# Second FFN: seven products for eight in the down projection, and low parts of weights made by transfers

## The chip, the cores and the metric

The kernel runs on one core of a Trainium2 chip. The metric is the device time of one execution in microseconds (us), the median of three runs. TensorE (PE) multiplies, VectorE (DVE) and ScalarE (ACT) work on tiles in SBUF and PSUM, GpSimd (POOL) works on SBUF tiles and issues transfers, and SyncE (SP) issues transfers.

## The reference, cut to what matters

One decoder layer on 544 tokens (a prompt of 512 and 8 x 4 sample tokens), all in float32, width 1024, hidden width 2816:

```python
def swiglu(x, w_gate, w_up, w_down):
    return (jax.nn.silu(x @ w_gate) * (x @ w_up)) @ w_down

x = x + 0.5 * swiglu(rms_norm(x, ffn1_norm), ffn1_gate, ffn1_up, ffn1_down)
z = rms_norm(x, mix_norm) @ w_in          # split among the heads of two mixers
x = x + concat(attention(z), gated_recurrence(z)) @ w_out
x = x + 0.5 * swiglu(rms_norm(x, ffn2_norm), ffn2_gate, ffn2_up, ffn2_down)
```

The attention is block-sparse, over a paged cache for the sample tokens (its pages are gathered by indirect transfers); the recurrence is computed in chunks.

## The kernel before, in words

Activations lie transposed: 8 tiles of 128 features x 544 tokens (`x` in the first FFN, `y` in the second), in two halves of 272 columns. A float32 product is made of three matmuls on rounded parts: every operand is split in a high part `hi` (a cast on ACT) and a low part `lo = src - hi` (a subtraction on DVE), and hi x hi, hi x lo and lo x hi are summed in PSUM (`products`). A matmul always has 128 rows, 128 columns of weights and 272 columns of tokens.

Weights come as jobs, in the order in which the products need them (`weight_jobs`). `w_load` loads raw pieces of 4 x 128 x 128 (256 KB; 192 KB where a group has 6 tiles) on SP's queue into slots `raw`, and `w_split` makes units (a pair `whi`, `wlo`) of them, at most `AHEAD` = 4 ahead of the products. There are 4 raw slots and 4 slots for pairs, and more from the time when the activations' own parts `xh`, `xl` are free (`more_slots`).

An FFN has 22 tiles of hidden features f, in groups of 8, 8 and 6 (`FGROUPS`). For f under 5 (`NREG`) gate and up are plain products: 8 k-tiles x 3 matmuls x 2 halves each, 48 matmuls. From f = 5 on, gate and up of one f are the two columns of a 2 x 2 block product, and seven products replace eight (`paired_gemm`; weights' sums `S`, two of them on DVE and two on POOL; token sums `xwh`, `xwl` made once by `right_factors`). Each of the seven takes 4 k-tiles x 3 matmuls, 84 matmuls for an f. After every group the down projection runs plainly over the group's hidden tiles (`hidden`, `split_hidden`: parts `hh`, `hl` or `xh`, `xl`), for 8 output tiles m in two halves, and adds half of the result to x. The last group's additions are followed by the output's transposes and stores (`store`).

Between the FFNs stand the 28 input projections (`project`), the mixers, and 8 output projections, whose weights come by the same jobs.

The order of instructions on each engine is written out before the kernel runs: `Order` holds a price for every instruction and transfer, gives each a planned start, and sorts every engine's queue by these starts (`give_out`). Each engine then works its queue strictly in that order and waits where an operand is late. All instructions are recorded by one helper, so the profile's line is always L284, and tiles' names tell them apart. In the second FFN the hidden parts and the extra weight slots share the names `xh` and `xl`.

At the start of the second FFN the residual `y` is read back from DRAM (`xs`) by eight transfers that POOL issues.

Of the kernel before, what the change touches and what calls it, by code (L numbers as in the profile page):

```python
# [30 lines left out]
FGROUPS = ((0, 8), (8, 8), (16, 6))  # L31
# [22 lines left out]
PACE = 0.8  # L54
# [124 lines left out]
class Engine:  # L179
# [22 lines left out]
    def __getattr__(self, op):  # L202
        real = getattr(self.real, op)

        def call(*args, **kw):
            names = list(self.tensors(args, kw))
            if op == "dma_start":
                s = self.order.dma(self.part, 4 * args[1].shape[0] * self.free(args[1]), names)
# [45 lines left out]
class Order:  # L254
# [103 lines left out]
    def dma(self, part, size, names, cost=0.06):  # L358
        s = self.fit(part, self.start(part, names), cost)
        e = self.fit("dma", s + cost + 1.5, size / 330e3) + size / 330e3  # L360
# [51 lines left out]

class Build:
# [34 lines left out]

    def weight_jobs(self):
# [7 lines left out]
        def plain(m, nk, r0, c0):  # L457
            out.append({"paired": False, "src": quarters(m, nk, r0, c0), "nk": nk // 2, "raw": [], "done": 0})

        def ffn(p):  # L460
            gate, up, down = (a[p + n][0] for n in ("_gate", "_up", "_down"))
            for g0, ng in FGROUPS:
                for f in range(g0, g0 + ng):
                    if f < NREG:
                        plain(gate, KD, 0, 128 * f)
                        plain(up, KD, 0, 128 * f)
                    else:
                        out.append({"paired": True, "nk": KD // 2, "raw": [], "done": 0,
                                    "src": quarters(gate, KD, 0, 128 * f) + quarters(up, KD, 0, 128 * f)})
                for m in range(KD):  # L470
                    plain(down, ng, g0, 128 * m)

        ffn("ffn1")
        for n, j in IN_ORDER:
            plain(a["w_in"][0], KD, 0, COLS[n] + 128 * j)
        for m in range(KD):
            plain(a["w_out"][0], KD, 0, 128 * m)
        ffn("ffn2")
        return out

    def room(self, kind, job):

        free = [x for x in self.slots[kind] if x["used"] < x["bufs"] and (x["extra"] is None or job["paired"])]
# [13 lines left out]
    def more_slots(self, pool):  # L497

        for i in range(KD):
            if i < 2:  # L500
                for t in ("xh", "xl"):
                    self.slots["raw"].append({"pool": pool, "tags": (f"{t}{i}",), "bufs": 1, "used": 0, "freed": [],
                                              "extra": pool})
            else:
                self.slots["w"].append({"pool": pool, "tags": (f"xh{i}", f"xl{i}"), "bufs": 1, "used": 0,
                                        "freed": [], "extra": pool})
# [9 lines left out]
    def w_load(self):  # L516
# [7 lines left out]
        self.nc.sync.dma_start(raw[:, :job["nk"]], job["src"][len(job["raw"])])  # L524
# [5 lines left out]
    def split_unit(self, src, nk, x):  # L530
        nc = self.nc
        hi, lo = self.take_slot(x, (F32R, F32R))
        nc.scalar.copy(hi[:, :nk], src[:, :nk])
        nc.vector.tensor_tensor(lo[:, :nk], src[:, :nk], hi[:, :nk].bitcast(F32), op=ALU.subtract)
        return hi, lo, x

    def w_split(self):
# [4 lines left out]
        if len(job["raw"]) <= (3 if job["paired"] else n):  # L542
            return False
        x = self.room("w", job)
        if x is None:
            return False
        nk = job["nk"]
        if job["paired"]:
            (a11, a12, a21, a22) = (r for r, _ in job["raw"])
            if n == 0:  # L550
                S = [self.tl(self.sums, [128, 4, 128], f"S{i}") for i in range(4)]
                for i, (e, p, q, op) in enumerate(((self.nc.vector, a21, a22, ALU.add),
                                                   (self.nc.vector, S[0], a11, ALU.subtract),
                                                   (self.nc.gpsimd, a11, a21, ALU.subtract),
                                                   (self.nc.gpsimd, a12, S[1], ALU.subtract))):
                    e.tensor_tensor(S[i][:, :nk], p[:, :nk], q[:, :nk], op=op)
                job["units"] = (a11, S[1], S[0], a12, S[2], S[3], a22)
            src = job["units"][n]
            self.units.append(self.split_unit(src, nk, x))
            drop = {0: (0, 2), 3: (1,), 6: (3,)}.get(n, ())  # L560
        else:
            self.units.append(self.split_unit(job["raw"][n][0], nk, x))
# [9 lines left out]
    def w_pump(self):  # L572
        while (len(self.units) < AHEAD and self.w_split()) or self.w_load():
# [69 lines left out]
    PAIRED = ((0, 0, True), (1, 4, True), (2, 3, True), (0, 1, False), (1, 5, False), (2, 2, False), (1, 6, False))  # L643

    def paired_gemm(self, xw, nk, evacs):
# [6 lines left out]
        for (b, r, first), evac in zip(self.PAIRED, evacs):  # L652
            w, = self.next_w(1)
            for k in range(nk):
                xh, xl = xw[k]
                self.products(ps[b], w, k, xh[:, r], xl[:, r], first and k == 0, k == nk - 1, not first)
# [4 lines left out]
    def right_factors(self, pool, x, gain):  # L661


# [4 lines left out]

        def lows(hi, lo, r, src):
            nc.scalar.copy(hi[:, r], src)  # L670
            nc.vector.tensor_tensor(lo[:, r], src, hi[:, r].bitcast(F32), op=ALU.subtract)

        def diff(out, p, q):
            nc.vector.tensor_tensor(out, p, q, op=ALU.subtract)

        for k in range(n):

            home, th, tl = self.hidden_home
            B1, B2, S1, S2 = [self.tl(home, [128, 2, HT], f"{t}{i}") for i in (6, 7) for t in (th, tl)]
            hi = self.tl(pool, [128, 7, HT], f"xwh{k}", F32R)  # L680
            lo = self.tl(pool, [128, 7, HT], f"xwl{k}", F32R)
            steps = [lambda B=B, m=m: nc.vector.scalar_tensor_tensor(
                B.rearrange("p a b -> p (a b)"), x[m], self.gains[:, gain, m:m + 1], self.R, op0=ALU.mult, op1=ALU.mult)
                for B, m in ((B1, k), (B2, k + n))]
            steps += [lambda a=a: diff(*a) for a in ((S1[:, 0], B1[:, 1], B1[:, 0]), (S1[:, 1], B2[:, 1], S1[:, 0]),
                                                     (S2[:, 0], B2[:, 1], B1[:, 1]), (S2[:, 1], B2[:, 0], S1[:, 1]))]
            steps += [lambda a=a: lows(hi, lo, *a) for a in ((slice(0, 1), B1[:, 0:1]), (slice(1, 3), B2),
                                                             (slice(3, 5), S1), (slice(5, 7), S2))]
            for step in steps:
                step()  # L690
                self.order.t = self.order.free["pe"] + PACE
                yield
            self.xw.append((hi, lo))
# [76 lines left out]

    def hidden(self, pool, i, hs):
# [4 lines left out]
        u = self.tl(pool, [128, T], "t_h", bufs=2)  # L776
# [8 lines left out]
        def up(p, h):  # L785
            c = self.cols(h)
            nc.vector.tensor_tensor(u[:, c], p, s[:, c], op=ALU.mult)
            if h:
                hs[i] = self.split_hidden(u, i)

        return gate, up

    def split_hidden(self, u, i):
        nc = self.nc
        pool, th, tl = self.hidden_home
# [1049 lines left out]
```

## Time and profile before

| what | value |
|---|---|
| median of 3 runs | 1205.38 us (1205.19 to 1206.52) |
| the profiled execution | 1210.65 us, span 1208.9 us |
| granted TensorE clock | 0.990 |
| PE busy | 1178.1 us, 97% of the span |
| DVE busy | 858.5 us, 71% |
| ACT busy | 551.9 us, 46% |
| POOL busy | 228.3 us, 19% |
| moved by DMA | 144.74 MB, mean 120 GB/s |

The span runs from the first to the last instruction of the program; the profiled execution's time has 1.75 us around it. Stages by the trace: first FFN to about 400 us, projections and mixers to about 785 us, output projection to about 826 us, second FFN from there to the end. The busy time of PE is that of pipelined matmuls; what a matmul costs is the distance from one to the next.

### The profile page before, as it was taken

The numbers are of one execution on the slowest core, as the hardware profiler recorded it, in microseconds if no ns is written. First come the engines' busy times: TensorE is split into PE (matmuls) and PEld (weight loads), VectorE is DVE, ScalarE is ACT, GpSimd is POOL, SyncE is SP. The second block draws the span as 40 slices with busy tenths as digits, with TensorE's granted clock in tenths as the row PEclk, the third lists the DMA queues.
The fourth block names the chain that finished last, engine by engine and source line by source line (L and its number), as shares of the span: only waits on it lengthen the run. The fifth ranks groups of instructions, "written<-read, shape, count | busy, mean of one in ns | idle before, by whom it ended". The sixth has DMA issues, their size and how long they took to land.

```text
span 1208.9 us, 26320 instructions
## 1 busy us (share of the span) xinstructions
PE 1178.1 (97%) x10571; PEld 1113.7 (92%) x10571; DVE 858.5 (71%) x1729; ACT 551.9 (46%) x1125; POOL 228.3 (19%) x211
## 2 busy tenths in 40 slices
PE   8999999999999999989999999899999999999998
PEld 8989999999999988878878867799999999999998
DVE  6988559954875698877776557667977488736843
ACT  6455246532654345554556433344554266524632
POOL 3012012200202401000332344220020023102200
PEclk9999999999999999989999999899999999999999
DMA  5244453333314642322565776352344323323222
GB/s 161 79 123 114 133 148 97 97 106 87 87 54 135 193 129 69 97 72 74 181 195 160 235 262 222 111 158 79 93 118 131 97 81 104 106 87 88 63 79 82
DMA packets 216238, 144.74 MB, mean 120 GB/s; under 512 B 12035, under 2 KB 204067, under 8 KB 216116
## 3 DMA queue, kind: packets, MB, share of 16 engines
q1 hardware_dynamic: 205588, 106.60, 30.6%
q0 software_dynamic: 10432, 36.32, 9.1%
q8 instruction: 83, 1.36, 0.5%
q14 instruction: 39, 0.32, 0.1%
q10 hardware_dynamic: 96, 0.14, 0.0%
HBM read 133.94 MB, written 11.83 MB: 121 GB/s over the span
## 4 chain that ended last, share of the span: by engine, by line
PE 77%; DVE 13%; ACT 3%; DMA 3%; issue 2%; SPq 1%; POOL 0%; DVEq 0%; ACTq 0%; POOLq 0%
PE mm L284 51%; PE sm L284 26%; DVE wlo L284 3%; DVE xl L284 2%; DVE xwl L284 1%; DMA raw<-ffn_down 1%; ACT xh L284 1%; DVE t_h L284 1%; SPq L284 1%; ACT whi L284 1%; DVE hl L284 1%; ACT sq L284 1%; DMA raw<-ffn_up 1%; DVE S L284 1%; DMA KV<-cache_v,idx 1%
## 5 line engine op out<-in xcount | busy, mean ns | idle before, releaser
L284 PE MATMUL mm<-xh,whi 128*128 128x272 f32 x1216 | 365.0, 300 | 1.0 <-DVE t_g L284 0.5
L284 PE MATMUL mm<-xl,whi 128*128 128x272 f32 x1216 | 352.4, 290 | 5.4 <-DVE xl L284 5.2
L284 PE MATMUL mm<-xh,wlo 128*128 128x272 f32 x1216 | 353.2, 290 | 1.1 <-DVE wlo L284 1.1
L284 ACT CAST whi<-raw 128x512 fp32r<-128x512 f32 (+1 forms) x230 | 138.7, 604 | 261.4 <-PE mm L284 192.3
L284 PEld LDWEIGHTS mm<-xh,whi 128*128 128x128 f32 x1216 | 231.5, 190 | 18.2 <-issue 15.7
L284 PEld LDWEIGHTS mm<-xl,whi 128*128 128x128 f32 x1216 | 231.3, 190 | 6.4 <-DVE xl L284 6.2
L284 PEld LDWEIGHTS mm<-xh,wlo 128*128 128x128 f32 x1216 | 231.0, 190 | 2.1 <-DVE wlo L284 2.1
L284 DVE TENSOR_TENSOR wlo<-raw,whi 128x512 fp32r<-128x512 f32 (+1 forms) x230 | 165.1, 727 | 81.0 <-ACT whi L284 77.4
L284 POOL TENSOR_TENSOR S<-raw,raw 128x512 f32<-128x512 f32 x18 | 30.4, 1691 | 380.9 <-DMA raw<-ffn_up 261.1
L284 PE MATMUL mm<-hh,whi 128*128 128x272 f32 x352 | 101.5, 288 | 0.3 <-DVE x L284 0.3
L284 PE MATMUL mm<-hh,wlo 128*128 128x272 f32 x352 | 101.1, 287 | 0.0
L284 PE MATMUL mm<-hl,whi 128*128 128x272 f32 x352 | 101.1, 287 | 0.0
L284 PE MATMUL mm<-xwh,xh 128*128 128x272 f32 x296 | 85.4, 288 | 1.3 <-DVE t_h L284 0.8
L284 PE MATMUL sm<-xwl,xh 128*128 128x272 f32 x296 | 85.3, 288 | 0.0
L284 PE MATMUL mm<-xwl,xh 128*128 128x272 f32 x296 | 85.3, 288 | 0.0
L284 PE MATMUL sm<-xwh,xh 128*128 128x272 f32 x296 | 85.2, 288 | 0.0
L284 PE MATMUL mm<-xwh,xl 128*128 128x272 f32 x296 | 85.2, 288 | 0.0
L284 PE MATMUL sm<-xwh,xl 128*128 128x272 f32 x296 | 85.2, 288 | 0.0
L284 DVE TENSOR_TENSOR xl<-S,xh 128x512 fp32r<-128x512 f32 x84 | 66.0, 796 | 4.1 <-ACT xh L284 3.7
L284 PEld LDWEIGHTS mm<-hh,whi 128*128 128x128 f32 x352 | 66.3, 188 | 0.7 <-ACT whi L284 0.5
L284 ACT CAST xh<-S 128x512 fp32r<-128x512 f32 x84 | 51.8, 620 | 32.7 <-DVE S L284 13.7
L284 PEld LDWEIGHTS mm<-hh,wlo 128*128 128x128 f32 x352 | 66.2, 188 | 0.0
(325 smaller groups left out, 2639.2 us busy)
## 6 DMA issues: line engine op xcount, KB each, us to landing
raw<-ffn_down SPq DMA_DIRECT2D x64, 256.0 KB
raw<-ffn_gate SPq DMA_DIRECT2D x56, 256.0 KB
raw<-ffn_up SPq DMA_DIRECT2D x56, 256.0 KB
raw<-w_in SPq DMA_DIRECT2D x56, 256.0 KB
raw<-ffn_down SPq DMA_DIRECT2D x32, 192.0 KB
xl<-ffn_gate SPq DMA_DIRECT2D x16, 256.0 KB
xh<-ffn_up SPq DMA_DIRECT2D x16, 256.0 KB
xl<-ffn_up SPq DMA_DIRECT2D x16, 256.0 KB
```

The costliest lines, as they stand in the source:

```text
L284: call(*map(real, args), **{k: real(v) for k, v in kw.items()})
```

## The change

Part by part:

1. **Down in seven products (second FFN alone).** Groups become 6, 6, 4, 6. Two hidden tiles (f, f + 1) by two token halves form the right 2 x 2 block, two output tiles m, m + 1 the left. `down_paired` adds each of the seven products' results to x as soon as it is complete. The class `Factors` holds the seven token factors, hi and lo, for a pair of hidden tiles, and makes them in steps: `first` after the even tile, `right` and `left` after the odd one.
2. **Another order of the seven.** `PAIRED` and the signs change, so that the factors appear in the order in which they are made. `right_factors` uses `Factors` too, two steps at a time (`PACE` 0.8 becomes 1.1).
3. **Weights' sums by transfers.** For every paired job a22 is added to a21 by an accumulating transfer that POOL issues (SBUF to SBUF); a21 + a11 is a POOL addition in the first FFN, and in the second a21 is loaded a second time and a11 is added to it by another such transfer. Two additions in place stay on DVE.
4. **Low parts by transfers.** For all weights of the input and output projections, for the second unit of each plain job of f under 5, and for the seventh unit of each paired job of the second FFN, ACT writes the negated source, rounded as `hi` is, into `lo`, and an accumulating transfer on POOL's queue adds the source to it. DVE has no part in it.
5. **Room and order.** 6 slots for pairs instead of 4, 6 units ahead instead of 4 in the projections, other extra slots; the first up product stays in PSUM; the residual is read back on SP's queue; the planner's prices for POOL's transfers change; the scratch for POOL's descriptors is set to 8192.

```diff
-FGROUPS = ((0, 8), (8, 8), (16, 6))
+FGROUPS = {True: ((0, 6), (6, 6), (12, 4), (16, 6)), False: ((0, 8), (8, 8), (16, 6))}
+AHEAD_MIX = 6
-PACE = 0.8
+PACE = 1.1
...
+class Factors:
+    def __init__(self, build, home, raw):
+        self.t = [build.tl(home(i)[0], [128, 2, HT], home(i)[1], F32R) for i in range(7)]
+        self.u = [build.tl(pool, [128, 2, HT], t) for pool, t in raw]
...
+    def split(self, hi, lo, raw):
+        return [lambda: self.nc.scalar.copy(hi, raw),
+                lambda: self.nc.vector.tensor_tensor(lo, raw, hi.bitcast(F32), op=ALU.subtract)]
...
+    def first(self):
+        return self.one(0, 0) + [self.diff(0, 1, 0)] + self.one(1, 0)
+    def right(self):
+        return [lambda: nc.vector.scalar_tensor_tensor(self.raw(0), self.raw(3), -1.0, self.raw(0),
+                                                       op0=ALU.mult, op1=ALU.subtract),
+                lambda: nc.vector.tensor_tensor(self.raw(1), self.raw(1), self.raw(3), op=ALU.add)] + self.two(2, 0)
+    def left(self):
+        return self.two(4, 2) + [self.diff(2, 2, 0)] + self.one(6, 2)
...
+        def paired(kind, nk, a11, a12, a21, a22, transfer):
+            job(kind, [a11, a21, a21 if transfer else None, a22, a12], nk)
...
+                for m in range(0, KD, 2):
+                    if pairs:
+                        paired("a", ng, *turns(down, ng, g0, 128 * m), *turns(down, ng, g0, 128 * (m + 1)), True)
...
+        if job["src"][i] is None:
+            self.nc.gpsimd.tensor_tensor(raw_k, parts[0], parts[1], op=ALU.add)
+        else:
+            self.nc.sync.dma_start(raw_k, job["src"][i])
+            if job["paired"] and i == 2:
+                self.nc.gpsimd.dma_start(raw_k, parts[0], accum_op=ALU.add)
+        if job["paired"] and i == 3:
+            self.nc.gpsimd.dma_start(parts[1], raw_k, accum_op=ALU.add)
...
         nc.scalar.copy(hi[:, :nk], src[:, :nk])
+        if transfer:
+            nc.scalar.activation(lo[:, :nk], src[:, :nk], AF.Identity, scale=-1.0)
+            nc.gpsimd.dma_start(lo[:, :nk], src[:, :nk], accum_op=ALU.add)
+            return hi, lo, x
         nc.vector.tensor_tensor(lo[:, :nk], src[:, :nk], hi[:, :nk].bitcast(F32), op=ALU.subtract)
...
+            if n in (1, 5):
+                out, p = (a11, s1) if n == 1 else (a12, a11)
+                self.nc.vector.tensor_tensor(out[:, :nk], out[:, :nk], p[:, :nk], op=ALU.add)
+            src = (a11, a11, s1, a12, s3, a12, a22)[n]
...
+            if last:
+                job["last"] = self.split_unit(a22, nk, xs[1], job["transfer"])
...
-    PAIRED = ((0, 0, True), (1, 4, True), (2, 3, True), (0, 1, False), (1, 5, False), (2, 2, False), (1, 6, False))
+    PAIRED = ((0, 0, True), (1, 2, True), (2, 1, True), (0, 4, False), (1, 3, False), (2, 5, False), (1, 6, False))
...
+    def down_paired(self, pool, x, m, done):
+        def add(m, c, ps, by=0.5):
+            nc.vector.scalar_tensor_tensor(x[m][:, c], ps, by, x[m][:, c], op0=ALU.mult, op1=ALU.add)
+        def p6(a, b, d):
+            nc.vector.tensor_tensor(b, b, s1, op=ALU.subtract)
+            add(m, r, b, -0.5)
+        def p3(a, b, d):
+            add(m, r, d, -0.5)
+            done(m)
+        def p4(a, b, d):
+            add(m + 1, l, b)
+            done(m + 1)
+        return (lambda a, b, d: nc.scalar.copy(s1, a), p6, lambda a, b, d: add(m + 1, r, d),
+                lambda a, b, d: add(m, l, a), lambda a, b, d: add(m + 1, r, b), p3, p4)
...
-                      "w": [{"pool": self.wp, "tags": ("whi", "wlo"), "bufs": 4, "used": 0, "freed": [], "extra": None}]}
+                      "w": [{"pool": self.wp, "tags": ("whi", "wlo"), "bufs": 6, "used": 0, "freed": [], "extra": None}]}
...
-                nc.gpsimd.dma_start(x[k], xspill[k])
+                nc.sync.dma_start(x[k], xspill[k])
...
-    nc = bacc.Bacc("TRN2", target_bir_lowering=False, num_devices=1)
+    nc = bacc.Bacc("TRN2", target_bir_lowering=False, num_devices=1, dynamic_dma_scratch_size=8192)
```

More of the change, by code (lines that the diff above doesn't have):

```diff
@@ L455, in quarters, with turns, job @@
                     for r in (r0, r0 + h)]
-        def plain(m, nk, r0, c0):
-            out.append({"paired": False, "src": quarters(m, nk, r0, c0), "nk": nk // 2, "raw": [], "done": 0})
-        def ffn(p):
+        def turns(m, nk, r0, c0):
+            rows = m[128 * r0:128 * (r0 + nk), c0:c0 + 128].rearrange("(k two p) m -> two p k m", two=2, p=128)
+            return [rows[0], rows[1]]
+        def job(kind, src, nk):
+            out.append({"kind": kind, "src": src, "nk": nk // 2, "raw": [], "done": 0, "paired": kind is not None, "mixer": False})
@@ L463, in ffn @@
                 for f in range(g0, g0 + ng):
                     if f < NREG:
-                        plain(gate, KD, 0, 128 * f)
-                        plain(up, KD, 0, 128 * f)
-                    else:
[L468 to L473, printed above, removed]
+                        plain(gate, KD, 0, 128 * f, start=True)
@@ L474, in weight_jobs @@
+        ffn("ffn1", False)
         for n, j in IN_ORDER:
-            plain(a["w_in"][0], KD, 0, COLS[n] + 128 * j)
+            plain(a["w_in"][0], KD, 0, COLS[n] + 128 * j, True)
         for m in range(KD):
-            plain(a["w_out"][0], KD, 0, 128 * m)
-        ffn("ffn2")
+            plain(a["w_out"][0], KD, 0, 128 * m, True)
+        ffn("ffn2", True)
         return out
     def room(self, kind, job):
-        free = [x for x in self.slots[kind] if x["used"] < x["bufs"] and (x["extra"] is None or job["paired"])]
+        free = [x for x in self.slots[kind] if x["used"] < x["bufs"] and x["extra"] in (None, job["kind"])]
@@ L495, in release, with more_slots @@
         self.order.done.update(t.name for t in tiles)
[L497 to L506, printed above, removed]
+    def more_slots(self, kind, pool, raws, parts):
+        for t in raws:
+            self.slots["raw"].append({"pool": pool, "tags": (t,), "bufs": 1, "used": 0, "freed": [], "extra": kind})
+        for t in parts:
+            self.slots["w"].append({"pool": pool, "tags": t, "bufs": 1, "used": 0, "freed": [], "extra": kind})
     def fewer_slots(self):
@@ L572, in w_pump, with ahead @@
     def w_pump(self):
-        while (len(self.units) < AHEAD and self.w_split()) or self.w_load():
+        def ahead():
+            mixer = self.splitting < len(self.jobs) and self.jobs[self.splitting]["mixer"]
+            return len(self.units) < (AHEAD_MIX if mixer else AHEAD)
+        while (ahead() and self.w_split()) or self.w_load():
             pass
@@ L654, in paired_gemm @@
             for k in range(nk):
-                xh, xl = xw[k]
-                self.products(ps[b], w, k, xh[:, r], xl[:, r], first and k == 0, k == nk - 1, not first)
+                f = xw[k]
+                self.products(ps[b], w, k, f.hi(r), f.lo(r), first and k == 0, k == nk - 1, not first)
                 yield
@@ L1046, in load_x @@
         ps = [[self.mm(), self.mm()], [self.sm(), self.sm()]]
-        out = [self.tl(pool, [128, T], t, bufs=2) for t in ("t_s", "t_h")]
+        out = self.tl(pool, [128, T], "t_s", bufs=2)
         LAG = 3
```

217 lines of the change are left out of this document (135 added, 82 removed).

## The prediction

> **What bounds the kernel now.** I read the page's busy times first, then stages, then the chain of waits, then rows of single operations.
>
> ```profile
> span 1208.9 us, 26320 instructions
> PE 1178.1 (97%) x10571; PEld 1113.7 (92%) x10571; DVE 858.5 (71%) x1729; ACT 551.9 (46%) x1125; POOL 228.3 (19%) x211
> ```
>
> PE fills 97% of the span, but this is an average. Stages (time, busy PE, PEld, DVE, ACT, POOL, clock, DMA share, GB/s):
>
> ```profile
> 60.00:100.00 40.00, 37.33 (x284) 35.67 (x283) 36.11 (x61) 20.74 (x41) 6.95 (x5) 1.00 0.43 113
> 430.00:500.00 70.00, 67.98 (x611) 60.25 (x611) 60.68 (x160) 37.20 (x88) 7.64 (x8) 1.00 0.32 93
> 500.00:580.00 80.00, 76.31 (x548) 66.41 (x548) 63.02 (x158) 39.09 (x91) 4.60 (x4) 0.91 0.26 75
> 580.00:660.00 80.00, 79.00 (x1151) 64.24 (x1150) 56.88 (x154) 42.64 (x110) 25.99 (x29) 1.00 0.60 183
> 700.00:785.00 85.00, 76.61 (x1171) 59.86 (x1172) 55.80 (x150) 27.18 (x75) 32.08 (x35) 0.96 0.59 197
> 785.00:826.00 41.00, 41.00 (x330) 41.00 (x329) 25.44 (x40) 18.37 (x31) 10.28 (x10) 1.00 0.48 144
> 978.60:1052.20 73.60, 73.60 (x589) 73.60 (x589) 64.06 (x103) 45.70 (x91) 21.07 (x12) 1.00 0.37 106
> 1052.20:1111.00 58.80, 58.80 (x472) 58.80 (x471) 28.43 (x50) 16.62 (x30) 5.50 (x4) 1.00 0.29 85
> ```
>
> The reader is to see three things. In the second FFN's gate and up (978.6 to 1052.2) PE never idles, while DVE is busy for 64.06 of 73.6 us, 87%. In its down (most of 1052.2 to 1111) DVE is at 48%. In the projections (430 to 785) PE has gaps although DVE is at 66 to 87%. The chain of waits (start, us, what) gives the price of a matmul:
>
> ```profile
> 989.10 10.49 PE mm L284 x84
> 1052.25 58.65 PE mm L284 x468
> ```
>
> 10.49 / 84 and 58.65 / 468 are both 125 ns, with no break where gate and up end and down begins. So there each matmul removed is worth 125 ns, unless something else becomes late.
>
> **The change: what it saves.** Down has 22 k-tiles x 8 outputs x 2 halves x 3 = 1056 matmuls. Seven for eight makes 924: per pair of outputs 63 in a group of 6 tiles (7.9 us), 42 in the group of 4 (5.25 us). 132 x 125 ns = **-16.5 us**. Nothing hides PE there, so all of it is gain until DVE steps in.
>
> **DVE in the new down.** Its operations have rows (gate and up window, last down, then a tile over the whole run with min/median/max):
>
> ```profile
> L284 DVE TENSOR_TENSOR wlo<-raw,whi 128x512 fp32r<-128x512 f32 x6 | 4.0, 682 | 0.0
> L284 DVE TENSOR_TENSOR xl<-t_h,xh 128x544 fp32r<-128x544 f32 x5 | 3.6, 726 | 0.6
> L284 DVE TENSOR_TENSOR t_h<-t_h,t_s 128x272 f32<-128x272 f32 x6 | 2.7, 443 | 3.0 <-ACT t_s L284 3.0
> L284 DVE TENSOR_TENSOR wlo<-raw,whi 128x384 fp32r<-128x384 f32 x12 | 6.7, 558 | 6.4 <-ACT whi L284 6.4
> L284 DVE SCALAR_TENSOR_TENSOR y<-mm,y 128x272 f32<-128x272 f32 x15 | 6.6, 442 | 12.0 <-PE mm L284 11.3
> L284 ACT CAST xh<-t_h 128x544 fp32r<-128x544 f32 x5 | 3.2, 650 | 0.9 <-DVE t_h L284 0.9
> L284 ACT ACTIVATE t_s<-sq 128x272 f32<-128x272 f32 x6 | 2.6, 431 | 1.6 <-DVE sq L284 1.6
> L284 ACT CAST whi<-raw 128x384 fp32r<-128x384 f32 x12 | 6.2, 513 | 15.9 <-PE mm L284 13.5 <-DVE wlo L284 2.4
> L284 DVE TENSOR_TENSOR xl<-S,xh x84: 675/684/1785, 85.2 to 1148.0; 128x512 fp32r<-128x512 f32 x84
> L284 POOL TENSOR_TENSOR S<-raw,raw x18: 1287/1673/2877, 78.9 to 1137.2; 128x512 f32<-128x512 f32 x18
> L284 POOL DMA_DIRECT2D y<-xs x8: 563/577/628, 782.7 to 786.5; - x8
> ```
>
> Per down product of a group of 6: six subtractions and two additions of 384 (8 x 0.558) and seven PSUM reads (7 x 0.442) are 7.6 us, against 7.9 of PE. In the group of 4 a piece has 256 elements; from 558 and 682 ns I extrapolate 434, so 8 x 0.434 + 3.1 = 6.6 us against 5.25: DVE is over by 1.3, for four products 5.2 us, of which units made ahead cover a part. ACT has eight casts of 0.513 and a copy, 4.5 us, and hides.
>
> Gate and up of the second FFN, per f: two additions and six subtractions (8 x 0.682 = 5.5), five PSUM operations (2.2), and the token factors, per two tiles three, then two, then two of 0.44 and twice 0.726, so 2.3 for one: 9.9 us against 10.5. DVE's cover shrinks from 13% to 5%, but stays. It stays because POOL's additions leave this FFN: beside them the same subtraction rises from 684 to at most 1785 ns. I put gate and up at 0 (ends 0 and +4).
>
> The Trainium skill, "SBUF — State Buffer", section "Who interferes with whom", states that a VectorE instruction with two SBUF inputs contends with a GpSimd instruction that reads SBUF, and not with one that only writes. These rows agree. By the rule, what POOL writes to issue the new transfers costs DVE nothing, and the sum is the one below. Were DVE blocked for every issue, 3 x 0.58 = 1.7 us for an f by the row of `y`, gate and up would need 11.6 us of DVE, 17 x 1.1 = 19 us more, and the sum would come out at +7; no row shows such a block.
>
> **Waits at two new places.** First, a down product's second factor comes from `right`, made after the sixth product of the last gate and up, 1.5 us before that ends: add 0.44, silu 0.43, multiply 0.44, two of 0.44, cast 0.65, subtraction 0.73, with an estimated 0.1 for each passing on some 4.2 us; the second product wants it 1.9 us after the end, so 4.2 - 1.5 - 1.9 = 0.8 us late, four times: **+3.2** (ends 0 and +8). Second, three PSUM banks serve the seven products, and the fifth product's result must be read before the seventh starts: one product between, 9 x 125 = 1.13 us (0.75 in the group of 4) against a read of 0.44 behind a DVE instruction under way of up to 0.56. I take 0.2 for each of 12 products and 0.9 for each of four, where the overload of 1.3 counts too: **+6** (ends 0 and +14).
>
> **The end.** The last two outputs finish together, so two sets of transposes and stores end it. Five transposes now take 0.55 us:
>
> ```profile
> 1199.21 0.55 PE sm L284 x5
> ```
>
> **+1** (ends 0 and +2).
>
> **Projections.** 72 subtractions leave DVE for ACT and POOL's queue. What that is worth:
>
> ```profile
> by line: PE mm L284 37.0%; PE sm L284 27.3%; DVE wlo L284 5.1%; issue 4.2%; DVE ms_qk L284 3.2%; DVE t_qk L284 3.0%; ACT sq L284 3.0%; DVE kn L284 3.0%; DVE y_qk L284 2.5%; DVE ql L284 1.8%; DVE z L284 1.6%; DVE kt L284 1.6%; ACT sc L284 1.
> by line: PE sm L284 48.8%; PE mm L284 31.6%; DMA KV<-cache_v,idx 3.2%; issue 3.2%; DVE sst L284 1.2%; ACT sq L284 1.2%; DVE xl L284 1.2%; ACT SC L284 1.0%; DVE rec L284 0.7%; DVE wlo L284 0.7%; DVE s L284 0.7%; ACT xh L284 0.6%; DVE hkh L28
> ```
>
> These are the chain's shares from 430 to 580 and from 580 to 785. `wlo` carries 5.1% of 150 and 0.7% of 205 us, together 9 us. Other DVE work takes its place in part; I take half: **-4.5** (ends -9 and +3). The second unit of the plain jobs leaves DVE too, where it is fullest (36.11 of 40 us from 60 to 100, PE idle 2.67): **-1** (ends -2.7 and +2).
>
> **Transfers.** No accumulating transfer stands in the trace; the nearest rows are the queues and POOL's issues:
>
> ```profile
> q1 hardware_dynamic: 205588, 106.60, 30.6%
> q0 software_dynamic: 10432, 36.32, 9.1%
> L284 POOL DMA_INDIRECT KV<-cache_k,idx x32 | 32.2, 1005 | 113.8 <-PE sm L284 61.6 <-DVE ql L284 44.5 <-PE mm L284 3.6
> ```
>
> Weight loads run at 106.6 MB in 30.6% of 1208.9 us, 288 GB/s; POOL's at 330. Gate and up: five loads of 262 KB are 4.6 us, three accumulations at one pass 2.4 us, together 7.0 of 10.5; at two passes 9.4; beyond 2.5 passes the transfers bind. In down the same pieces shrink with the products. POOL issues three per product, 0.58 to 1.0 each, 1.7 to 3 us, which fits. The change adds a chain to every paired job: load, accumulation, addition on DVE, cast, subtraction. If the accumulation is late, the addition stands at the head of DVE's queue, and behind it stand the PSUM reads that free PE's banks. What hides it is room: 14 raw slots (4, and 10 of `xh`, `xl`) at five a job start the loads nearly three jobs, over 20 us, early. On POOL a late load holds up the low parts queued behind its accumulation, by the same cover. So I put transfers at 0 (ends 0 and the second rival below). The Trainium skill, "DMA: Bandwidth & Descriptors", section "Issuing engines are not separate DMA queues", speaks against the change here: issuing from POOL adds no bandwidth. It is the reason that I added the loads and the accumulations; no run here shows the accumulation's price.
>
> The residual on SP's queue saves POOL eight issues of 0.58 us. On SP they wait for the mixers' memory as they did on POOL, and weight loads planned after them wait behind them; PE is busy for 41.00 of 41 us there (785 to 826) on weights loaded earlier, so 0 (ends -1 and +2).
>
> **Edits at nothing.** In the first FFN one POOL addition per f becomes a transfer and the products stay; DVE's next idle time covers it. The first up product, read from PSUM, saves two DVE copies at 28 us while PE works on the next product. `right_factors` does the same kind of work in other steps, within the plain gate and up that cover it now. Other group sizes cost no matmul.
>
> **Sum.** -16.5 + 3.2 + 6 + 1 - 4.5 - 1 = -11.8 us. Against the profiled execution, 1210.65 us (the span and 1.75 around it), that is 1198.9; its median stands 5.3 us lower, so 1205.4 - 11.8 = 1193.6, **1194 us**.
>
> **Rivals.** *DVE is the bound of the whole second FFN* (0.14). 17 x 9.9 + 12 x 7.6 + 4 x 6.6 = 286 us of DVE against 294 of PE. Every wait of DVE on ACT or PE must then fit in 8 us; if 12 us of waits show on PE beside my 10, the saving is used up: about 1205, 1201 to 1208. For it: 95% and 96%. Against: at 87% PE lost nothing.
>
> *POOL's queue makes low parts late: slower* (0.14). POOL works in order, and gathers wait in it:
>
> ```profile
> POOL KV L284 <- PE sm L284: 101.6, 48, 11.2
> 702.71 6.53 DMA KV<-cache_v,idx
> ```
>
> A gather waited up to 11.2 us, and 6.53 us passed on the chain until one landed. A low part queued behind such a gather comes that much late. Six units ahead, less the two in use, are two projections of 6 us: 12 us of cover. The wait alone fits, wait and landing (17.7) do not. Each caught job costs about 6 us; with three caught it eats the gain, with five the kernel takes 1194 + 30 = 1224; I say 1208 to 1225. Against: the waits are for PE, which also delays the use.
>
> *The projections gain all* (0.10): DVE at 80% is what stretches them, and the planner's order closes up; with -9 there, and no waits in down, 1205.4 - 16.5 - 9 + 1 - 1 = 1180, 1174 to 1184.
>
> **How the numbers follow.** My forecast has 0.62, from 1184 to 1202. About 0.2% (2.4 us) is what a measurement can tell. Range 1182 to 1208: it leaves out most of the slower rival and of the last. Faster: 0.62 - 0.01 + 0.10 + 0.04 of the first rival, 0.75; same 0.11; slower 0.14.
>
> **What would show it.** Matmuls of `y`'s down fall by 132; the chain shows 63 and 42 per product at 125 ns. Gaps of PE at four group starts would name DVE's last factor, and in the third down DVE would be at 95% or more. If the projections take as long as before (430 to 785), my -4.5 is wrong. Wrong altogether would be PE waits for DMA `whi` or `wlo` (POOL's queue), or DMA shares above 0.9 in the second FFN.

## The result, and the profile after

| | before | after |
|---|---|---|
| median | 1205.89 us | 1220.26 us (1216.80 to 1222.14) |
| ratio to before | 1 | 1.0116, interval 1.0088 to 1.0144 |
| span of the profiled execution | 1208.9 us | 1220.2 us |
| matmuls | 10571 | 10439 |

The kernel became 1.2% slower where I forecast 1.0% faster. The 132 matmuls are gone. Over all sessions three executions lay far off the rest (before 1410 and 6342 us, e13 below 4737 us); the medians count them, the ratios do not. The page after, its busy times, the DMA engines' share in 40 slices, and the queues:

```profile
PE 1168.5 (96%) x10439; PEld 1102.6 (90%) x10439; DVE 841.2 (69%) x1866; ACT 652.3 (53%) x1369; POOL 329.4 (27%) x358
DMA  6566454453324984855886999464578979969873
q1 hardware_dynamic: 221860, 116.17, 33.1%
q0 software_dynamic: 39456, 84.17, 32.5%
```

PE is busy for 10 us less and the span is 11 us longer: PE waits. DVE, which I watched, is busy for less than before. ACT and POOL are each busy for 100 us more, but far from full. What grew most is the fourth line: POOL's queue of transfers went from 9.1% to 32.5% of all 16 DMA engines.

Stages tell where. Every 272-column matmul stands in the trace in the kernel's order, so counting them gives each stage's first matmul; a stage lasts from its own to the next one's, the last stage to the start of the last such matmul. Profiled executions, in us:

| stage | before | after | matmuls alone (125 ns each) |
|---|---|---|---|
| first FFN, plain gate and up | 70.2 | 68.5 | 60 |
| first FFN, first three paired products | 34.2 | 39.5 | 31.5 |
| rest of the first FFN | 282.7 | 282.0 | 279 |
| input projections and mixers | 367.6 | 357.0 | |
| output projection | 56.8 | 73.2 | 48 |
| second FFN, plain gate and up | 63.8 | 64.1 | 60 |
| second FFN, rest | 316.6 | 319.4 | 310.5 before, 294 after |

The border between the input projections and the output projection moves with the planned order: between the output projection's first matmul and the second FFN's first stand 9 smaller matmuls of the mixers before, and 105 after. So of these two stages the sum is the safer reading: 424.4 us before, 430.2 after. By itself the output projection's 16.4 us are 8.8 of more idle PE (13.3 for 4.5 us) and 7.6 of more busy PE, with those mixers' matmuls in it and a granted clock of 0.88 for 0.94.

The second FFN's rest, after, piece by piece: first paired product 18.8 (10.5 of matmuls), down 34.1 (31.5), gate and up 63.5 (63), down 32.1 (31.5), gate and up 42.0 (42), short down 24.6 (21), gate and up 68.6 (63), last down 35.8 (31.5 and some 4 of output transposes).

The largest loss at one place, in the output projection. Chain of waits after (start, us, what), POOL's low part for an output weight first:

```profile
785.00 5.34 DMA wlo<-raw
...
790.40 0.37 SPq L288
...
791.06 0.34 SPq L288
...
791.45 3.20 DMA y<-xs
...
794.80 0.45 DVE y L288
...
795.30 4.90 PE mm L288 x20
```

The residual's reads in the same execution, by tile (ns min/median/max, first and last start):

```profile
L288 SPq DMA_DIRECT2D y<-xs x8: 338/430/646, 791.1 to 794.5; - x8
```

And two rows of PE's waits from 790 to 925 (total, times, longest):

```profile
PE mm L288 <- DVE y L288: 8.9, 1, 8.9
PE sm L288 <- ACT whi L288: 5.3, 2, 4.5
```

A raw piece's slot is free when the accumulating transfer that reads it has landed, here after 5.3 us. The next load of an output weight waits for that slot on SP, the eight reads of y stand behind that load on the same queue, the addition to y waits for them, and with it PE's banks: 8.9 us. Before, y was issued at 782.7, after at 791.1. The second wait is the second FFN's first paired product, where the chain shows a load that is late:

```profile
895.00 1.52 PE sm L288 x12
...
899.46 5.38 DMA raw<-ffn_gate
904.84 0.02 issue
904.86 0.63 ACT whi L288
```

PE's products run dry in the middle of the stage, the load that starts at 899.46 lands at 904.84, and only then can its cast start. The stage's window, after, and that of the same product in e13 (below), where nothing is late (time, busy PE, PEld, DVE, ACT, POOL, clock, DMA share, GB/s):

```profile
894.80:913.60 18.80, 13.10 (x87) 12.22 (x86) 9.82 (x19) 7.86 (x19) 4.63 (x6) 0.91 0.98 230
881.90:892.40 10.50, 10.50 (x86) 10.50 (x85) 9.46 (x20) 6.28 (x16) 3.46 (x4) 1.00 1.00 268
```

Of the 8.3 us lost, PE is idle for 5.7 and busy for 2.6 more on the same matmuls, at a granted clock of 0.91 instead of 1.00. So a stage with a wait lost more than the wait; that the wait lowered the clock was not tested. Behind the short down it is the same kind of chain, through a low part and the load that got its slot:

```profile
1110.87 7.08 DMA wlo<-xl
1117.97 6.78 DMA xl<-ffn_gate
1124.85 0.62 ACT xh L288
```

with the DMA engines full or nearly so (columns as above; the profile's share can read above 1):

```profile
1011.00:1043.00 32.00, 31.77 (x254) 31.55 (x253) 29.08 (x65) 18.09 (x39) 10.18 (x12) 1.00 0.97 214
1109.80:1120.00 10.20, 10.20 (x83) 10.19 (x82) 8.42 (x16) 5.63 (x12) 5.10 (x6) 1.00 1.14 258
1120.00:1140.00 20.00, 17.22 (x123) 16.46 (x122) 12.26 (x24) 11.12 (x24) 4.30 (x5) 0.91 0.92 203
```

In the second down DVE is busy for 29.08 of 32 us and PE loses 0.6 us: DVE at 91% is no bound there. From 1120 to 1140 DVE is at 61%, DMA at 0.92, and PE loses 2.8 us and, at a granted clock of 0.91, some of its speed.

### The profile page after: what moved, and what is told of

Its sections match the earlier page's. It is cut to its first block, busy times and chain, and to the rows that moved or that the text cites. A ratio compares the mean times of both kernels' runs of the same rounds, so it can differ in the third digit from the quotient of the medians.

```text
span 1220.2 us, 26922 instructions
## 1 busy us (share of the span) xinstructions
PE 1168.5 (96%) x10439; PEld 1102.6 (90%) x10439; DVE 841.2 (69%) x1866; ACT 652.3 (53%) x1369; POOL 329.4 (27%) x358
## 3 DMA queue, kind: packets, MB, share of 16 engines
q0 software_dynamic: 39456, 84.17, 32.5%
## 4 chain that ended last, share of the span: by engine, by line
PE 74%; DVE 8%; DMA 7%; issue 4%; ACT 3%; POOL 2%; SPq 1%; POOLq 0%; ACTq 0%; DVEq 0%
PE mm L288 46%; PE sm L288 29%; DMA KV<-cache_v,idx 2%; DVE xl L288 1%; DVE U L288 1%; DMA raw<-w_in 1%; POOL KV L288 1%; DMA wlo<-raw 1%; DMA raw<-ffn_gate 1%; ACT xh L288 1%; DVE xh L288 1%; SPq L288 1%; DMA wlo<-xl 1%; DVE hw L288 1%; DVE xw L288 1%
## 5 line engine op out<-in xcount | busy, mean ns | idle before, releaser
L288 ACT CAST whi<-raw 128x512 fp32r<-128x512 f32 (+2 forms) x233 | 139.3, 600 | 170.6 <-PE mm L288 106.1
L288 PE MATMUL mm<-hw,whi 128*128 128x272 f32 x737 | 141.3, 288 | 0.8 <-DVE hw L288 0.8
L288 PE MATMUL sm<-xw,whi 128*128 128x272 f32 x648 | 125.0, 291 | 7.7 <-ACT whi L288 5.3
L288 PE MATMUL mm<-xw,whi 128*128 128x272 f32 x648 | 124.3, 290 | 1.0 <-ACT t_g L288 1.0
L288 DVE TENSOR_TENSOR wlo<-raw,whi 128x512 fp32r<-128x512 f32 (+2 forms) x141 | 94.0, 673 | 39.2 <-ACT whi L288 37.2
L288 PEld LDWEIGHTS mm<-hw,whi 128*128 128x128 f32 x737 | 116.0, 188 | 1.7 <-DVE hw L288 1.5
L288 PEld LDWEIGHTS sm<-xw,whi 128*128 128x128 f32 x648 | 102.8, 191 | 8.6 <-ACT whi L288 5.7
L288 PEld LDWEIGHTS mm<-xw,whi 128*128 128x128 f32 x648 | 102.3, 190 | 1.2 <-ACT t_g L288 1.2
L288 PE MATMUL mm<-hw,wlo 128*128 128x272 f32 x358 | 102.9, 287 | 0.0
L288 PE MATMUL sm<-xw,wlo 128*128 128x272 f32 x324 | 94.3, 291 | 0.4 <-DVE wlo L288 0.4
```

Of the source, the lines that this page charges most:

```text
L288: call(*map(real, args), **{k: real(v) for k, v in kw.items()})
```

## The experiments

Theory A: transfers hold slots and queues, and the order on SP makes it worse. Rival B: the transfers in flight are the cost themselves, whatever the order. Rival C: DVE is the bound. The kernel before took 1206 to 1211 us in the sessions, so each kernel is compared by its ratio to before.

**e1: the residual back on POOL's queue.**

```diff
-                nc.sync.dma_start(x[k], xspill[k])
+                nc.gpsimd.dma_start(x[k], xspill[k])
```

> The changed kernel with one edit undone: the residual y is read back on POOL's queue again, not on SP's. Theory A (SP's queue works in order, and the eight reads stand behind loads of output weights whose slots are free only when a low part's transfer has landed): the output projection's stage, 73.2 us in the changed kernel and 56.8 before, falls by 9 to 13 us, and the time from 1220 to 1207 to 1211. Rival B (the low parts' transfers make that stage late whichever queue reads y): the stage falls by 3 us at most, 1217 to 1220.

Measured 1218.57 us, ratio 1.0108 (1.0082 to 1.0135). The output projection took 71.5 us, both stages together 425.0, 5.2 less than after, but the ratio fell by 0.0008 alone. So the order on SP was not the cause by itself: PE is still idle for 6.5 us in one piece there, because on POOL the reads stand behind the low parts themselves (from 740 to 800 us POOL waited up to 19.3 us for ACT's part of one of them). Theory A falls at this place in its simple form.

**e2: two more raw slots for paired jobs.**

```diff
+        self.more_slots("a", wide, [f"rawx{i}" for i in range(2)], [])
...
-    nc = bacc.Bacc("TRN2", target_bir_lowering=False, num_devices=1, dynamic_dma_scratch_size=8192)
+    nc = bacc.Bacc("TRN2", target_bir_lowering=False, num_devices=1, dynamic_dma_scratch_size=4096)
```

> The changed kernel with two more slots for raw pieces of paired jobs, there from the start of each FFN (the room comes from a descriptor scratch of 4096 instead of 8192). Theory A (the first paired job needs five slots and has four; the fifth load waits for a slot and is issued behind up to ten loads of later jobs): the first paired stage falls from 39.5 to about 34 us in the first FFN and from 18.8 to about 12 in the second; time 1207 to 1212. Rival B (the transfers in flight, not the order, make the load late): each stage falls by 2 us at most, 1216 to 1220. If the smaller scratch slows POOL's issues, all later stages grow.

Measured 1213.99 us (1206.00 to 1217.61), ratio 1.0038 (1.0012 to 1.0063). The first paired stages took 37.3 and 17.7 us, 2 and 1 less, as B expected. Even these are hardly the slots' gain: in e1, e3 and e5, which lack them, the first of these stages took 37.6 to 37.8 us too. The time lies between the two theories, and its executions spread over 11.6 us; the profiled one took 1217.42 us, so the profile doesn't show where the fast ones gained. The chain of e2 at the second FFN's first paired product: a load of 6.06 us still stands in it, and then an accumulation and the addition behind it.

```profile
896.23 6.06 DMA xl<-ffn_down
...
903.01 3.09 DMA raw<-xh
...
906.19 0.56 DVE raw L288
```

**e3: all projections' low parts by DVE again** (the flag dropped from both lines of `weight_jobs`).

> The changed kernel with the low parts of input and output projection weights made by DVE again (six slots and six units ahead stay). If the 10.7 us gained in the projections come from the offload, their stage goes from 357 back to 366 to 369 us; if they come from the six units ahead, it stays at 357 to 360. The output projection's stage falls by 8 to 14 us because raw slots come free sooner and y is read sooner. Time 1206 to 1222, by the first part.

Measured 1210.37 us, ratio 1.0026 (1.0010 to 1.0042). The output projection fell to 55.6 us, with y still on SP, issued at 779.1 (e3, by tile):

```profile
L288 SPq DMA_DIRECT2D y<-xs x8: 338/431/602, 779.1 to 782.5; - x8
```

The input projections took 361.0, so 4 of the 10.7 us gained went back at most, but the border moved. Both together took 416.6 us, against 424.4 before and 430.2 after.

**e4: plain down in the second FFN** (`ffn("ffn2", False)` and the same flag in `ffn2`; with it the second FFN's weights' sums are made as in the first, one by POOL and one by a transfer, and the seventh low part by DVE).

> The changed kernel without the seven products in down: groups 8, 8, 6 and plain down in the second FFN, whose weights' sums are made as in the first (one POOL addition, one transfer); all else stays. The second FFN from its first paired product on takes 319.3 us in the changed kernel and 316.6 before. Theory A (the seven products cost as much in waits as they save): 314 to 320 us, time 1216 to 1222. Rival B (their transfers are what made the kernel slower): below 310 us, time under 1212. Rival C (they save most of 16.5 us, and the loss is elsewhere): over 325 us, time over 1226.

Measured 1221.11 us, ratio 1.0112 (1.0093 to 1.0130). The second FFN's rest took 322.0 us: with the seven products it was 319.4, so 2.6 of 16.5 us were left on balance, between A and C. By pieces the balance is a gain and a loss: with the seven products the downs took 9.6 us less (126.5 for 136.1), and gate and up 6.9 more (192.8 for 185.9), 5.3 of it behind the short down. Its first three paired products took 38.3, 5 more than before: that loss is not the seven products'.

**e5: only the output projections' low parts by DVE.**

```diff
-            plain(a["w_out"][0], KD, 0, 128 * m, True)
+            plain(a["w_out"][0], KD, 0, 128 * m)
```

> The changed kernel with the low parts of the eight output projections' weights alone made by DVE; the input projections keep theirs by transfers. Theory A (a raw slot that a low part's transfer holds until it has landed delays the next load and, behind it on SP, the read of y; that is the whole loss of the output projection): its stage falls from 73.2 to 55 to 58 us, the input projections stay at 354 to 358, time 1201 to 1206. Rival B (transfers of the input projections, still in flight, are part of it): the stage stays over 62 us, time over 1208.

Measured 1212.40 us, ratio 1.0017 (1.0002 to 1.0032). The output projection took 57.5 us, as A expected. But the input projections took 364.2, not 357, because the border moved back (9 mixers' matmuls again). The sum is 421.6, 8.6 under the changed kernel's and 2.8 under before's, and PE's idle time in the output projection is back to 3.9 us: shown, without the low parts of the eight output weights the two stages lose nothing against before. The time missed A's range even by the ratio: 1208 us where before takes 1205.9.

**e6, e7, e8: on e5, fewer transfers in two ways, and another order of groups.** e6 makes a21 + a11 of the second FFN by POOL and the seventh low part by DVE (transfer flag off); e7 makes both sums by POOL additions in both FFNs; e8:

```diff
-FGROUPS = {True: ((0, 6), (6, 6), (12, 4), (16, 6)), False: ((0, 8), (8, 8), (16, 6))}
+FGROUPS = {True: ((0, 6), (6, 6), (12, 6), (18, 4)), False: ((0, 8), (8, 8), (16, 6))}
```

> Output projection's low parts on DVE, and the second FFN's paired jobs with one accumulating transfer instead of three: a21 + a11 is a POOL addition (no second load of a21), the seventh low part is DVE's. If the transfers are the bound of the second FFN (DMA shares of 0.84 to 1.14 there), its stages from the first paired product on fall from 319 to 305 to 312 us, and time is 1194 to 1200. If DVE is the bound, one more subtraction for each product and POOL's additions beside it make them 325 to 340 us, time over 1210.

> Output projection's low parts on DVE, and both sums of weights' pieces as POOL additions in both FFNs; low parts by transfer stay. Theory A (at the first paired product of each FFN the chain load, accumulation, addition is what is late: 5 to 6 us and 3.2 us): those stages fall by 3 to 5 us each, from 39.5 and 18.8 to 35 and 15. Rival B (DVE bound): with two POOL additions per product beside DVE, which the trace of before showed to stretch a subtraction from 684 to up to 1785 ns, the second FFN's later stages grow by 5 to 20 us. Time 1195 to 1215.

> Output projection's low parts on DVE, and groups 6, 6, 6, 4 instead of 6, 6, 4, 6. In the changed kernel the down of the group of 4 takes 24.6 us for 21 us of matmuls, and the gate and up after it 68.6 for 63. Theory A (in the short group DVE and the transfers fall behind, and the next group's loads are late): with no group behind it the 5.6 us go, and the last down takes 24 to 27 us with its transposes: time 1196 to 1201. Rival B (the 5.6 us come from elsewhere): the last gate and up still loses 4 us or more, time 1202 to 1207.

Measured: e6 1228.19 us, ratio 1.0152 (1.0123 to 1.0181), second FFN's rest 337.2; e7 1249.57 us, ratio 1.0329 (1.0285 to 1.0374), 352.9; e8 1207.02 us, ratio 0.9962 (0.9944 to 0.9980), 316.8. DVE's subtractions in e7's second FFN, by tile:

```profile
L288 DVE TENSOR_TENSOR wlo<-raw,whi x44: 410/683/1810, 899.8 to 1231.0; 128x512 fp32r<-128x512 f32 x27, 128x384 fp32r<-128x384 f32 x12, 128x256 fp32r<-128x256 f32 x5
```

The same in the changed kernel:

```profile
L288 DVE TENSOR_TENSOR wlo<-raw,whi x44: 411/680/693, 905.5 to 1200.8; 128x512 fp32r<-128x512 f32 x27, 128x384 fp32r<-128x384 f32 x12, 128x256 fp32r<-128x256 f32 x5
```

And e7's stretch as a whole, first as a window, then as the shares of its chain:

```profile
891.30:1244.20 352.90, 323.19 (x2389) 307.81 (x2387) 291.25 (x547) 188.52 (x412) 106.95 (x96) 0.98 0.43 107
```

```profile
by line: PE sm L288 29.7%; PE mm L288 19.8%; DVE wlo L288 10.2%; DVE U L288 8.1%; DVE xl L288 5.7%; DVE xh L288 4.6%; issue 4.2%; ACT xh L288 3.4%; DVE y L288 3.3%; ACT xl L288 2.5%; DVE hw L288 1.9%; ACT whi L288 1.8%; DMA raw<-ffn_down 1.
```

With POOL's additions a subtraction takes up to 1810 ns, without them 693 at most in this row, while POOL issues more transfers; DVE's work grows to 291 us, the DMA share falls to 0.43, and half of the chain leaves PE, for DVE's subtractions (`wlo`, `xl`, `xh`) and products' sums (`U`) first. e7 lies beyond both ranges that I gave. So C holds for these variants: without the transfers the seven products wait for DVE (e6: 293 us of 337.2). The rule of the Trainium skill's "SBUF — State Buffer" (section "Who interferes with whom"), weighed in the prediction, agrees with these rows: beside additions, which read SBUF, a subtraction was stretched; beside issues alone it was not (693 ns).

In e8 no gate and up stands behind the short group, and its 5.6 us are gone; the last down took 26.3, as A expected, and the time by the ratio, 1201 us, is at the end of A's range. But the gate and up behind the first down took 68.3 us, 5.3 over its matmuls, by loads that take 7 to 9 us to land and an accumulation of 5.9 (the chain of e8):

```profile
923.40 9.21 DMA xh<-ffn_up
...
933.71 5.85 DMA raw<-xl
...
943.90 7.28 DMA xl<-ffn_up
```

**e9 and e10: put together.** e9 is e2, e3 and e8 in one. e10 also makes the sums of each FFN's first paired job by DVE, without an accumulating transfer and without the second load of a21:

```diff
-                        paired("a", KD, *quarters(gate, KD, 0, 128 * f), *quarters(up, KD, 0, 128 * f), pairs)
+                        paired("a", KD, *quarters(gate, KD, 0, 128 * f), *quarters(up, KD, 0, 128 * f), pairs and f > NREG)
+                        out[-1]["first"] = f == NREG
...
-            self.nc.gpsimd.tensor_tensor(raw_k, parts[0], parts[1], op=ALU.add)
+            (self.nc.vector if job.get("first") else self.nc.gpsimd).tensor_tensor(raw_k, parts[0], parts[1], op=ALU.add)
...
+            if job.get("first"):
+                self.nc.vector.tensor_tensor(parts[1], parts[1], raw_k, op=ALU.add)
```

> Low parts of all projection weights by DVE (as in e3), two more raw slots for paired jobs (as in e2), groups 6, 6, 6, 4 (as in e8). If the three losses are separate, their ratios multiply: e3 1.0026, e2 against the changed kernel 0.992, e8 against e5 0.9945, together 0.989, about 1193 to 1197 us where before is at 1207. If they are one loss (transfers in flight) seen at three places, taking one away eases the others and the sum is smaller: ratio 0.994 to 0.999.

> As e9, and the first paired job of each FFN makes both sums on DVE and its seventh low part too, without an accumulating transfer. Theory (at the first paired product the chain load, accumulation 3 to 6 us, addition ends last): the two first stages, 37 to 39 and 18 us, fall by 3 us each, time 5 us under e9. Rival (the loads themselves, many released at once, are late): no difference, within 2 us of e9.

Measured: e9 1206.43 us, ratio 0.9958 (0.9940 to 0.9977): not the product of the three. That fits the second half of the expectation, one loss seen in part at three places; but e2's ratio, on executions that spread over 11.6 us, may also have been too good, and the runs don't tell the two apart. e10 1204.68 us, ratio 0.9941 (0.9921 to 0.9962), 2 us under e9; the first stages took 38.0 and 15.7 us, 0.3 and 1.8 less. So by the time the rival came true. In the second FFN the wait moved on to the second paired job, again a load and an accumulation (the chain of e10):

```profile
889.78 4.32 DMA xl<-ffn_down
...
894.12 3.71 DMA rawx<-raw
```

**e11: e3 with 4 slots and 4 units ahead** (`bufs` 6 to 4, `AHEAD_MIX` 6 to 4).

> As e3 (low parts of projections by DVE), but 4 slots for pairs and 4 units ahead, as before the change. e3's input and output projections together took 416.6 us, before 424.4, changed 430.2. If the room and the six units ahead made that gain, they go back to 422 to 427 us and time to 1214 to 1220; if not, they stay at 415 to 419, time 1208 to 1213.

Measured 1224.31 us, ratio 1.0099 (1.0069 to 1.0128). The projections together took 423.2 us. That is the expected number, but e12, whose order up to the second FFN is e3's, took 420.9, so 4 us is what two profiles of the same work can differ by, and the projections' part in it is not settled. The first FFN shows the room more clearly: its plain part took 71.2 us instead of 68.5 and its first paired stage 42.3 instead of 37.8.

**e12: e3 without the accumulations in the second FFN's paired jobs.**

```diff
-            if job["paired"] and i == 2:
-                self.nc.gpsimd.dma_start(raw_k, parts[0], accum_op=ALU.add)
...
-        if job["paired"] and i == 3:
+        if job["paired"] and i == 3 and not job["transfer"]:
```

> As e3, but the second FFN's paired jobs leave out the two accumulating transfers that make the weights' sums (so these sums are wrong there; the loads, the additions on DVE and all products stay). It measures the transfers' time at an unchanged DVE load. If the DMA engines are the bound in the second FFN, its stages from the first paired product on fall from 321 us (e3) to 300 to 308, and DMA shares there from 0.85 to 1.0 to under 0.7. If DVE is the bound, they fall by 4 us at most.

Measured 1205.29 us, ratio 0.9960 (0.9945 to 0.9976). Its second FFN leaves two terms out of the weights' sums and so computes other values, with the same work on DVE and PE. The second FFN's rest took 312.1 us instead of 324.3. e3's window (both windows end 6 us before the stage does):

```profile
880.70:1199.00 318.30, 303.39 (x2340) 298.03 (x2339) 257.92 (x541) 188.78 (x413) 82.48 (x96) 0.98 0.82 185
```

and e12's:

```profile
884.50:1190.60 306.10, 297.30 (x2340) 294.45 (x2339) 257.13 (x538) 188.09 (x411) 27.19 (x32) 0.99 0.57 145
```

So 12 us of that stretch are the accumulations' (7 against the changed kernel's 319.4). It lies between the two theories, and the pieces tell where: the gate and up behind the short down took 63.6 us, its matmuls and 0.6, for 70.0 in e3, and the first down 32.1 for 34.1; the first paired product stays at 18.2 us, so what is late there is the load.

**e13 and e14: what was still open.** e13 is e10 with the second paired job of each FFN made by DVE too; e14 is e10 with plain down.

> As e10, and the second paired job of each FFN (the sixth gate and up of the first, the first down of the second) also makes its sums on DVE and its seventh low part too. Theory (load, then 3 to 4 us of accumulation, then addition, is what ends last there): the first paired stage of the first FFN falls from 38.0 to 34 to 35.5 us, that of the second from 15.7 to 12 to 14; time 4 to 6 us under e10 (ratio 0.989 to 0.991). Rival (loads released all at once land late whatever follows): within 2 us of e10.

> As e10 without the seven products in down (groups 8, 8, 6, eight products). e10's second FFN from its first paired product on takes 309 us, before 316.6. If the seven products are worth what shows there, this one takes 316 to 319 us and the time is 6 to 10 us over e10 (ratio 0.999 to 1.003). If the gain of e10 is in the other edits, both are within 3 us.

Measured: e13 1197.11 us, ratio 0.9921 (0.9901 to 0.9941), the fastest of all; e14 1204.60 us, ratio 0.9987 (0.9971 to 1.0002). In e13 the second FFN's first paired product took 10.5 us, its matmuls alone, and the rest as a whole 304.5; in e10 309.9; in e14 318.3. The stretch in e13:

```profile
881.90:1186.40 304.50, 301.08 (x2383) 298.31 (x2382) 259.95 (x546) 187.41 (x409) 79.97 (x93) 1.00 0.83 188
```

e10 and e14 differ by 8.4 us of the stage, 5.5 by the ratios, but not in the seven products alone: as in e4, e14's second FFN makes its weights' sums as the first FFN does. With the second job mended too (e13, an edit that e14 doesn't have) it is 13.8 of the stage, 8.0 by the ratios. The pieces, added up, keep the two apart:

| second FFN's rest, us | gate and up | down |
|---|---|---|
| before, plain down | 180.5 | 136.1 |
| e4, plain down | 185.9 | 136.1 |
| e14, plain down | 182.2 | 136.1 |
| after | 192.8 | 126.5 |
| e12, no accumulations | 187.5 | 124.6 |
| e10 | 184.6 | 125.3 |
| e13 | 179.4 | 125.1 |
| e6, fewer transfers | 200.9 | 136.3 |
| e7, fewer transfers | 212.6 | 140.3 |

Plain down took 136.1 us in three kernels, the seven products 126.5 in the changed one and 125.1 in e13: 9.6 to 11 of the 16.5 us were there from the start. What hid them is the gate and up, 12.3 us longer after than before, and in e13 no longer so. The DMA share in e13 is 0.83, as in the changed kernel (0.82 from 892.5 to 1214.7), and 1.00 in its first product, where PE is busy all the time: in these runs the share by itself cost little, and what cost was a product that stood right behind a late load and an accumulation.

By the ratios e13 is 2.4 us under e10, less than the 4 to 6 expected. In the first FFN the expectation missed: 39.5 us, where e10 took 38.0 and before 34.2. The chain of e13 there shows a plain load that is late, with no accumulation behind it:

```profile
82.80 5.00 DMA raw<-ffn_up
...
87.92 0.70 DVE rawx L288
```

DVE's addition waits for it, the reads of PE's banks stand behind that addition, and PE waits 3.7 us; the stage's granted clock is 0.91, before 1.00. So the rival, loads that land late whatever follows, is what this trace shows for the first FFN. No run removes this loss, so its cause is read from one chain and not tested.

## Why the prediction was wrong, point by point

- *What it saves, -16.5.* Right in kind: 132 matmuls at 125 ns. The downs took 9.6 us less than before, in e13 11.0; the rest of the 16.5 went to the waits of the next point.
- *DVE in the new down, and the waits at two places, +9.2.* About right in size, in part by luck. The four downs lost 2.6, 0.6, 3.6 and about 0.4 us, 7.2 together; the short one the 4 x 0.9 that I put there, and e12, without the accumulations, lost as much there. But of the first one's 2.6 e12 lost 0.6 alone, so 2 of them are the transfers' and not DVE's last factor. *Gate and up at 0* held for DVE: 63.5 and 42.0 us for 63 and 42.
- *Transfers at 0.* This is the step that failed. I bounded an accumulation between one and two passes, worked out that two passes make 9.4 of 10.5 us, and took 0 because 14 slots start the loads early. The size was at the far end: between the changed kernel and e3 72 transfers of 262 KB less took the queue from 32.5% of 1220.2 us to

```profile
q0 software_dynamic: 29088, 65.29, 24.1%
```

  of 1211.0 us (e3's queues), 104.7 us for 72, 1.45 us each on all engines, 1.8 passes at the 330 GB/s of POOL's queue before. It is the time that packets took beside other traffic, so waits within the engines are in it. At such a share the loads in the chains above landed after 4 to 9 us and the accumulations after 3 to 7. The cover failed at each place where it isn't there: at the second FFN's first paired product (8.3 us lost; gone in e13), behind the short down (5.6; 0.6 in e12), and, by loads alone as far as e13's trace shows, in the first FFN (5.3, and 3.1 at least in every run). With the output projection (next point) that is over 20 us at places where I had put 0. The first jobs there start from four slots, not 14; but two more slots (e2) hardly helped. That the Trainium skill's "DMA: Bandwidth & Descriptors" (section "Issuing engines are not separate DMA queues") spoke against the change was right: the share of all 16 engines rose with POOL's queue. I used it only for the sum of bytes.
- *Slots.* I counted a low part's price on ACT, POOL and DVE, but not the time for which its transfer keeps the raw slot: landing took 4.1 us in the median (transfers of the changed kernel: KB each, us from issue to landing).

```profile
wlo<-raw POOLq DMA_DIRECT2D x91, 256.0 KB, 4.1
```

  That cost PE 8.9 us in one wait and the two projection stages 8.6 in their sum (e5).
- *The residual on SP's queue, 0.* Right by itself: undoing it in e1 moved the ratio by 0.0008, and in e3 y on SP came early. I named "weight loads planned after them"; the ones ahead of them counted.
- *Projections, -4.5.* Low parts by transfers gave nothing that can be told: the two stages together took 420 to 422 us in e5 to e8 but e6's 418.6, with the input weights' low parts by transfers, and 415.8 to 422.6 with all on DVE (e3, e9, e10, e12 to e14). The changed kernel's chain from 430 to 460 us shows a wait of their kind there as well: a low part landed after 5.46 us, the load that got its slot after another 12.06, and PE was idle for 5.3 us soon after.
- *The first plain part, -1, and the end, +1*: -1.7 and +0.4.
- *Rivals.* Slower came true, by slots and late loads and not by gathers ahead in POOL's queue; no low part behind a gather stands in the chains above. DVE became the bound only where transfers were taken away (e6, e7). A DMA share above 0.9 in the second FFN, named as the sign of a wrong forecast, showed.

## What to carry to other kernels

When work moves from an engine to a transfer, price three things: the DMA engines' time, the landing time at the share that results, and the time for which the transfer keeps its source's buffer from the next load. A depth of buffers covers only the steady state; where a stage starts with few buffers, the first jobs can be made by an engine that has time there, as in the second FFN of e13. Read experiments by stages and their pieces, and check that a stage's border stayed where it was: here losses of 3 to 9 us at four places hid a saving that was there.

## What the runs showed of the hardware

An accumulating transfer of 256 KB from SBUF to SBUF took 1.45 us of all 16 DMA engines, some 180 GB/s, against 330 for the gathers of before, and those of 192 and 256 KB landed after 3.1 to 7.1 us in the rows of the chains above. Its issue on POOL took 0.93 us in the mean (count, busy us, mean ns, idle before; after's groups):

```profile
L288 POOL DMA_DIRECT2D wlo<-raw x92 | 83.1, 931 | 225.5 <-ACT wlo L288 186.4
```

That is not the accumulation's own price: a plain load that POOL issued took 0.58 us before and 1.0 in e1 (medians of the eight reads of y). Beside such issues DVE's subtractions took 693 ns at most in the row of `wlo`, beside POOL's additions up to 1810 ns.

In e13's first product of the second FFN the DMA engines' share was 1.00 and PE lost nothing; in the changed kernel's, at 0.98, it lost 8.3 us. Where PE waited the granted clock was lower too: 0.91 in that stage and 0.88 in the output projection after, against 1.00 in e13's first product. That the wait causes it was not tested.
